# A decoder mixer kernel: the first merge gate computed as two sets of seven block products, with sums of weight blocks made by accumulating transfers

## Chip, cores and metric

The kernel runs on one core of a Trainium2 chip. Its time is the device time of one execution in microseconds (us), and lower is better. Three runs of the kernel before gave a median of 1141.31 us (1141.27 to 1141.62).

## The reference, cut to what matters

One decoder layer on 256 tokens of width 2048. The normed input is projected by `w_in`; the columns give a gated linear attention (q, k, v, gate), a differential attention (q, k, v, gate) and two merge gates `m_a` and `m_b`. Everything is float32.

```python
h = rmsnorm(x, pre_norm_g[l])
proj = h @ w_in[l]
(a_q, a_k, a_v, a_g, a_lr, b_q, b_k, b_v, b_g, m_a, m_b) = jnp.split(proj, offsets, axis=-1)
...                                     # o_a, o_b: the two mixers' gated outputs, 256 x 2048 each
y_a = o_a @ w_branch_a[l]
y_b = o_b @ w_branch_b[l]
merged = jax.nn.sigmoid(m_a) * y_a + jax.nn.sigmoid(m_b) * y_b
out = merged @ w_out[l]
x = x + rmsnorm(out, post_norm_g[l])
```

The change concerns `m_a = h @ W` with W of 2048 x 2048, four column groups of 512 named m00 to m03.

## The kernel before

All weights are read once from DRAM, in one flat array `w` laid out in the order of use (`chunk_plan`). A load brings 1 MB (128 partitions x 2048 numbers) into one of three `raw` buffers, issued on SP's queue. Each half of it (1024 numbers a partition) is a *unit*: ScalarE rounds it to fp32r (`hi`, L162), VectorE subtracts to get the rest (`lo`, L163), both into rings of three buffers. TensorE then computes three products for each block of 128 rows: x_hi·w_hi, x_lo·w_hi and x_hi·w_lo. x is split once into the `xs` tiles and stays.

`take` hands TensorE the next unit and keeps the splits and their loads up to AHEAD = 4 units in front. `token_major` (L304) computes a group of 512 columns for all 256 tokens: x blocks are the stationary operand, the weights stream by 512 columns, 8 steps of 12 matmuls into two PSUM banks (one for each 128 tokens). Work of other kinds (the two attentions, transposes) is written as generators in `tasks`; `pump` puts a piece of them between steps. A scheduler at build time then fixes each engine's order. Instructions of one engine run in that order, and so do SP's transfers: a transfer that waits for a buffer holds all behind it.

The order of the stages is: values v, keys and queries of the linear attention, its gate `ag`, the heads of the differential attention 0 and 1 (`diff_heads`), then for each g the gate m0g and the branch product y0g, heads 2 and 3, the gate groups m10 to m13, y10 to y13 (which read the attention outputs `obh` and `obl`, the hi and lo parts), then o0 to o3. Before, m0 and y0 make `part` (L771). After y1g VectorE forms (1 + tanh)·y_b + part in the gate's tile (L800, L801), and `turn` (L784) transposes it (L791) for the output product. Long-lived tiles come from one pool `big` of 4 KB slots that are reused in turn. GpSimd computes the attention's small rsqrt (`de`, L248) and a few memsets (L607).

Of the kernel before, what the change touches and what calls it, by code (L numbers as in the profile page):

```python
# [6 lines left out]
F32 = mybir.dt.float32  # L7
# [23 lines left out]
def chunk_plan():  # L31

    plan = []
    at = 0
    for g, n in enumerate(VG):
        if g == 0:
            plan.append(("v0", "two", "w_in", [(6144, RANK), (2048, 2 * n - RANK)]))
            at = 2 * n - RANK
        elif g > 1:
            plan.append((f"v{g}", "tok", "w_in", [(2048 + at, n)]))  # L40
            at += n
    for hf in range(2):
        for name, base in (("k", 1024), ("q", 0)):
            for c in range(4):
                plan.append((f"{name}{hf}{c}", "chan", "w_in", [(base + 512 * hf + P * c, P)]))
    for g in range(4):
        plan.append((f"ag{g}", "tok", "w_in", [(4096 + 512 * g, 512)]))
    o = 6144 + RANK

    def heads(g):  # L50
        plan.append((f"dv{g}", "tok", "w_in", [(o + 4096 + 512 * g, 512)]))
        plan.append((f"bg{g}", "tok", "w_in", [(o + 6144 + 512 * g, 512)]))
        for pair in range(2):
            for n, name in enumerate(("dq", "dk")):
                for c in (2 * pair, 2 * pair + 1):
                    plan.append((f"{name}{g}{c}", "chan", "w_in", [(o + 2048 * n + 512 * g + P * c, P)]))

    def gate(br, g):
        plan.append((f"m{br}{g}", "tok", "w_in", [(o + 8192 + 2048 * br + 512 * g, 512)]))

    def branch(br, g):
        plan.append((f"y{br}{g}", "tok", ("w_branch_a", "w_branch_b")[br], [(512 * g, 512)]))

    heads(0)
    heads(1)
    for g in range(4):
        gate(0, g)
# [7 lines left out]
    for g in range(4):  # L75
        plan.append((f"o{g}", "tok", "w_out", [(512 * g, 512)]))
    return plan


@with_exitstack  # L80
def hybrid_kernel(ctx: ExitStack, tc, xt, xn, preg, postg, w, w2, gkb, glag, lamv, diffg, ident_d, causal_d, lmask_d, out):
# [22 lines left out]

    def ps(tag):
        count[0] += 1
        return psum.tile([P, 512], F32, tag=tag, name=f"{tag}_{count[0]}")

    def f32(ap):
        return ap.bitcast(F32)  # L110


    plan = chunk_plan()
    halves = []
    off = 0
    for key, kind, _, cols in plan:
        n = sum(c for _, c in cols)
        size = ROWS[kind] * n
        for _ in range(KT // ROWS[kind]):
            halves += [(key, off, size, 0), (key, off, size, 1)]  # L120
            off += size * P
    ready = {}
    emitted = [0]
    raws = {}

    def emit_half():
        j = emitted[0]
        emitted[0] += 1
        key, at, size, h = halves[j]
        if h == 0:  # L130
            raws[at] = wpool.tile([P, 2048], F32, tag="raw", name=f"raw_{at}")
        raw = raws[at]
        src = w[at : at + P * size].rearrange("(p n) -> p n", p=P)
        n = size // 2
        early = key == "v0"
        if h == 0:
            if j == 0:
                load_x(0, 1)
            cuts = (0, n, size) if j == 0 else (0, size)
            for a, b in zip(cuts, cuts[1:]):  # L140
                i = sp.dma_start(raw[:, a:b], src[:, a:b])
# [11 lines left out]
        if key == "o3" and j + 1 < len(halves):  # L153
            hi_t, lo_t = u([P, 1024], "keep", F32R), u([P, 1024], "keep", F32R)
        else:
            hi_t = wpool.tile([P, 1024], F32R, tag="hi", name=f"hi_{j}")
            lo_t = wpool.tile([P, 1024], F32R, tag="lo", name=f"lo_{j}")
        fine = 2 if j == 0 else 1
        for i in range(fine):
            a, b = n * i // fine, n * (i + 1) // fine  # L160
            r = raw[:, n * h + a : n * h + b]
            act.activation(hi_t[:, a:b], r, AF.Copy)  # L162
            dve.tensor_tensor(out=lo_t[:, a:b], in0=r, in1=f32(hi_t[:, a:b]), op=ALU.subtract)  # L163
        ready[j] = (key, hi_t, lo_t)
# [3 lines left out]
    def take(key):  # L168
        j = used[0]
        used[0] += 1  # L170
        while emitted[0] < min(j + 1 + AHEAD, len(halves)):
# [130 lines left out]
        return i.ins  # L302

    def token_major(key, n, ops, step=1, groups=1):  # L304
        banks = [[ps(tag), ps(tag)] for tag in ("mm", "bg")[:groups]]
        spots = [(g, b) for g in range(groups) for b in range(2)]
        rows = 2 // groups
        for q in range(KT // rows):
            hi, lo = take(key)
            for w, parts in ((hi, (0, 1)), (lo, (0,))):  # L310
                for j in range(rows):
                    kt = rows * q + j
                    a = ops(kt)
                    for g, b in spots:
                        c = n * (groups * j + g)
                        for part in parts:
                            first, last = kt == 0 and w is hi and part == 0, kt == KT - 1 and w is lo
                            i = pe.matmul(banks[g][b][:, :n], a[part][:, P * b : P * b + P], w[:, c : c + n], start=first, stop=last)  # L318
            latest[0] = i.ins
            if groups == 1 and q % 2:  # L320
                pump(step)
            if groups == 2 and q == KT - 4:
                with tc.issue_after(latest[0]):
                    norm()
            if groups == 2 and q > 10:
                pump()
        return banks if groups == 2 else banks[0]

    def channel_major(key):
# [265 lines left out]


    obh, obl = [], []

    def diff_split(g, pair, tq, tk, q2, kh, kl):
        for m in range(2):  # L600
# [74 lines left out]
    def diff_attention():  # L675
# [3 lines left out]
        while n < 16 or last or pair:  # L679
# [24 lines left out]
                act.activation(new["wt"], new["bank"][:, :384], AF.Copy)  # L704
            if pair:
                split_out(bank, hi, lo, diffg_s)
                pair = None
            if last:
                if last["h"] % 2 == 0:
# [5 lines left out]
            if n == 16:  # L715
                yield

    def diff_heads(g):
# [8 lines left out]
        obh.append(u([P, 4, S], "obh", F32R))  # L727
        obl.append(u([P, 4, S], "obl", F32R))
        for pair in range(2):
            ts = []  # L730
            for name in ("dq", "dk"):
                t = t2([P, 2, S], name)
# [18 lines left out]
    def b_ops(kt):  # L751
        return obh[kt // 4][:, kt % 4, :], obl[kt // 4][:, kt % 4, :]

    def merge_gate(br, g, dst):
        banks = token_major(f"m{br}{g}", 512, x_ops, 1 + br)
        for b in range(2):
            act.activation(dst[:, b, :], banks[b], AF.Tanh, scale=half_rstd[:, b : b + 1])

    tasks.append(diff_attention())
    diff_heads(0)  # L760
# [1 line left out]

    while not {"out0", "out1"} <= done:
        pump()
    part = [u([P, 2, 512], "part") for _ in range(4)]
    for g in range(4):
        t = u([P, 2, 512], "mgate")
        merge_gate(0, g, t)
        banks = token_major(f"y0{g}", 512, a_ops)
        for b in range(2):  # L770
            dve.scalar_tensor_tensor(out=part[g][:, b, :], in0=t[:, b, :], scalar=1.0, in1=banks[b], op0=ALU.add, op1=ALU.mult)  # L771

    diff_heads(2)
    diff_heads(3)

    gb = [u([P, 2, 512], "gateb") for _ in range(4)]
    for g in range(4):
        merge_gate(1, g, gb[g])
    while tasks:
        pump()  # L780
    mh = [u([P, 4, S], "mh", F32R) for _ in range(4)]
    ml = [u([P, 4, S], "ml", F32R) for _ in range(4)]

    def turn(g):  # L784
        yield
        for i in range(2):
            bank = ps("bg")
            for j in range(2):
                for b in range(2):
                    c = P * (2 * i + j)  # L790
                    pe.transpose(bank[:, P * (2 * j + b) : P * (2 * j + b) + P], gb[g][:, b, c : c + P], ident)  # L791
            hi = mh[g][:, 2 * i : 2 * i + 2, :].rearrange("p a t -> p (a t)")
            lo = ml[g][:, 2 * i : 2 * i + 2, :].rearrange("p a t -> p (a t)")
            split_out(bank, hi, lo, 0.5)

    for g in range(4):
        banks = token_major(f"y1{g}", 512, b_ops)
        for b in range(2):
            t = gb[g][:, b, :]
            dve.scalar_tensor_tensor(out=t, in0=t, scalar=1.0, in1=banks[b], op0=ALU.add, op1=ALU.mult)  # L800
            dve.tensor_tensor(out=t, in0=t, in1=part[g][:, b, :], op=ALU.add)  # L801
        tasks.append(turn(g))
# [135 lines left out]
```

## Time and profile before

| what | value |
|---|---|
| median of three runs | 1141.31 us |
| profiled execution, span | 1139.5 us; its time outside the span is not recorded |
| TensorE, matmul / weight load | busy 1127.4 / 971.0 us, 5698 each |
| VectorE / ScalarE / GpSimd | busy 700.7 / 602.5 / 49.1 us |
| DMA | 211.60 MB, 53.2% of the 16 engines' span on SP's queue |

A matmul's busy time overlaps with that of its neighbours, so the time of one is read from the length of a long piece of the chain divided by its count. In the page's groups a row gives line, engine, operation, out<-in, count, busy us, mean ns of one, and then the idle time ahead of it with the engine it waited for.

### The profile page before, as it was taken

What the parts mean: (1) busy time and instruction counts of PE and PEld (TensorE: products, weight loads), DVE (VectorE), ACT (ScalarE), POOL (GpSimd) and SP (SyncE); (2) the same over time, 40 slices, a digit from 0 to 9 for tenths busy, and PEclk for the clock granted to TensorE, in tenths of its full rate; (3) what the DMA queues carried; (4) which work ended last, traced back from release to release, by engine and by line L of the source; (5) the groups of instructions that cost most, each with busy time, mean ns of one, the idle gap of its engine ahead of it and who ended that gap; (6) DMA issues with size and microseconds to landing.
All of it is one profiled execution on the core that took longest, in us unless ns stands there. A gap on an engine that the chain in (4) does not pass through costs nothing.

```text
span 1139.5 us, 14734 instructions
## 1 busy us (share of the span) xinstructions
PE 1127.4 (99%) x5698; PEld 971.0 (85%) x5698; DVE 700.7 (61%) x1025; ACT 602.5 (53%) x902; POOL 49.1 (4%) x61
## 2 busy tenths in 40 slices
PE   9999999999999999999999999999999999999997
PEld 8999888888888888888888888888888888888886
DVE  7765588657857766766444454676577544566454
ACT  7675454545646665665444434576466544444451
POOL 0100031001100000000000000000000000000000
PEclk9999999999999999999999999999999999999999
DMA  8756555545455445545555555554554555556762
GB/s 320 228 187 222 185 173 174 197 164 192 141 181 183 147 154 181 185 148 185 185 189 201 200 185 188 187 180 148 185 185 148 174 196 185 185 188 207 275 217 74
DMA packets 32742, 211.60 MB, mean 186 GB/s; under 512 B 4192, under 2 KB 4832, under 8 KB 10144
## 3 DMA queue, kind: packets, MB, share of 16 engines
q1 hardware_dynamic: 31952, 209.61, 53.2%
q10 hardware_dynamic: 720, 1.06, 0.3%
q8 instruction: 44, 0.72, 0.3%
q14 instruction: 26, 0.21, 0.1%
HBM read 208.55 MB, written 2.10 MB: 185 GB/s over the span
## 4 chain that ended last, share of the span: by engine, by line
PE 97%; issue 1%; ACT 1%; DMA 0%; DVE 0%; SPq 0%; DVEq 0%; POOLq 0%; POOL 0%; ACTq 0%
PE mm L318 65%; PE mm L339 15%; PE mm L341 8%; PE bg L318 1%; PE mm L301 1%; PE bg L508 1%; PE bg L301 1%; PE bg L624 1%; PE bg L625 1%; DMA raw<-in_w_dram 0%; PE bg L650 0%; ACT kh L605 0%; PE bg L791 0%; PE bg L577 0%; ACT kh L604 0%
## 5 line engine op out<-in xcount | busy, mean ns | idle before, releaser
L163 DVE TENSOR_TENSOR lo<-raw,hi 128x1024 fp32r<-128x1024 f32 (+3 forms) x386 | 467.7, 1214 | 347.3 <-ACT hi L162 344.4
L162 ACT ACTIVATE hi<-raw 128x1024 fp32r<-128x1024 f32 (+3 forms) x386 | 401.5, 1042 | 459.3 <-PE mm L318 338.3
L318 PE MATMUL mm<-hi,xs 128*128 128x512 f32 (+2 forms) x1536 | 373.0, 384 | 1.4 <-ACT hi L162 1.4
L318 PEld LDWEIGHTS mm<-hi,xs 128*128 128x128 f32 x1536 | 285.6, 188 | 50.6 <-ACT hi L162 2.0
L318 PE MATMUL mm<-lo,xs 128*128 128x512 f32 (+2 forms) x768 | 201.5, 382 | 0.0
L339 PE MATMUL mm<-xs,hi 128*128 128x512 f32 x768 | 195.6, 393 | 0.0
L318 PEld LDWEIGHTS mm<-lo,xs 128*128 128x128 f32 x768 | 143.8, 188 | 25.6 <-DVE lo L163 0.3
L339 PEld LDWEIGHTS mm<-xs,hi 128*128 128x128 f32 x768 | 138.4, 189 | 24.2
L341 PEld LDWEIGHTS mm<-xs,lo 128*128 128x128 f32 x768 | 104.8, 190 | 7.5
L341 PE MATMUL mm<-xs,lo 128*128 128x256 f32 x768 | 107.1, 282 | 0.0
L318 PE MATMUL mm<-hi,obh 128*128 128x512 f32 x128 | 50.1, 391 | 0.0
L318 PE MATMUL mm<-hi,oah 128*128 128x512 f32 x128 | 49.9, 390 | 0.0
L318 PE MATMUL mm<-hi,obl 128*128 128x512 f32 x128 | 49.8, 389 | 0.0
L318 PE MATMUL mm<-hi,oal 128*128 128x512 f32 x128 | 49.8, 389 | 0.0
L635 ACT ACTIVATE prob<-prob,mx,score_scale 128x128 f32<-128x128 f32 x64 | 34.3, 537 | 7.8 <-DVE mx L630 7.2
L318 PE MATMUL mm<-hi,mh 128*128 128x512 f32 x96 | 37.5, 390 | 0.0
L318 PE MATMUL mm<-hi,ml 128*128 128x512 f32 x96 | 37.4, 389 | 0.0
L318 PE MATMUL mm<-lo,oah 128*128 128x512 f32 x128 | 34.2, 389 | 0.0
L318 PE MATMUL mm<-lo,obh 128*128 128x512 f32 x128 | 34.2, 389 | 0.0
L248 POOL TENSOR_TENSOR de<-de,neg_half 128x2 f32<-128x2 f32 x16 | 11.8, 738 | 395.8 <-DVE de L669 395.8
L318 PEld LDWEIGHTS mm<-lo,oah 128*128 128x128 f32 x128 | 24.0, 188 | 5.0
L318 PEld LDWEIGHTS mm<-lo,obh 128*128 128x128 f32 x128 | 24.0, 188 | 5.0
(194 smaller groups left out, 984.9 us busy)
## 6 DMA issues: line engine op xcount, KB each, us to landing
raw<-in_w_dram SPq DMA_DIRECT2D x176, 1024.0 KB, 4.9
raw<-in_w_dram SPq DMA_DIRECT2D x15, 832.0 KB, 6.4
raw<-in_w_dram SPq DMA_DIRECT2D x4, 800.0 KB, 4.5
xres<-in_xn_dram SPq DMA_DIRECT2D x4, 512.0 KB, 10.2
xraw<-in_xt_dram SPq DMA_DIRECT2D x3, 512.0 KB, 8.0
lmask<-in_lmask_dram SPq DMA_DIRECT2D x2, 512.0 KB, 7.6
pg<-in_postg_dram SPq DMA_DIRECT2D x2, 512.0 KB, 6.7
out_dram<-yg SPq DMA_DIRECT2D x4, 256.0 KB, 2.7
```

The lines of the kernel that those rows point to most:

```text
L162: act.activation(hi_t[:, a:b], r, AF.Copy)
L163: dve.tensor_tensor(out=lo_t[:, a:b], in0=r, in1=f32(hi_t[:, a:b]), op=ALU.subtract)
L248: pool.tensor_tensor(out=dst, in0=src, in1=neg_half[:, : src.free_size()], op=ALU.pow)
L301: i = pe.matmul(out, lhs, rhs, start=first and n == 0, stop=last and n == len(pairs) - 1)
L318: i = pe.matmul(banks[g][b][:, :n], a[part][:, P * b : P * b + P], w[:, c : c + n], start=first, stop=last)
L339: i = pe.matmul(o, hi[:, c], x_pair(kt), start=kt == 0, stop=kt == KT - 1)
L341: i = pe.matmul(o[:, :S], lo[:, c], x_ops(kt)[0], start=False, stop=False)
L508: pe.matmul(o, xk[:, P * c : P * c + P], xq.rearrange("p (b c t) -> p b c t", b=2, c=4)[:, :, c, :], start=i == 0, stop=i == 1)
L624: pe.matmul(banks[m][:, lo:up], q2[:, m, i2, t], kh[:, m, i2, :n], start=True, stop=False)
L625: pe.matmul(banks[m][:, lo:up], q2[:, m, i2, t], kl[:, m, i2, :n], start=False, stop=True)
L635: act.activation(prob[m][:, lo:up], prob[m][:, lo:up], AF.Exp, scale=score_scale[:, b : b + 1], bias=mx[:, i : i + 1], accum_out=z[:, i : ...
```

## The change

The gate m0 is no longer computed group by group. Two column groups form a *set* of 1024 columns. The weights of a set are cut into 2 x 2 blocks of 1024 rows x 512 columns, x into 2 x 2 blocks of 128 tokens x 1024 channels, and the 2 x 2 block product is formed by seven block products in place of eight (`PRODUCTS`). Each product is four units of 1024 numbers with 6 matmuls a unit, all into one bank.

The seven need sums of x blocks and of weight blocks. The x sums are made once on VectorE and split (`block_operands`, a task during the last heads). The weight sums are made in memory: two *chains* of four tiles. A chain tile is loaded from DRAM by SP; after its unit was split, a transfer issued by GpSimd adds the next weight block onto it (`accum_op=ALU.add`). Chain 0 serves products 1, 3, 5 and 7, chain 1 products 2 and 6, and in the second set the two swap. Product 4 uses a plain block, loaded as two raw tiles. A transfer is issued eight units ahead (`load_block(i + 8)`). Results of the products are combined on VectorE and ScalarE (`block_set`), and the two sets' 56 steps are interleaved with the 32 steps of m10 to m13 (`schedule`, `mixed`).

With the gate moved behind the heads, y0g is computed by itself and copied to `part` by ScalarE; the tiles `part`, `obh` and `obl` are written to DRAM by GpSimd's queue and read back by SP before y1. `part` is multiplied by the gate just after y1's products. All PSUM tiles now share one ring of eight banks, `big` has 34 slots, and the memory that GpSimd's transfers use for their descriptors is set to 4096 bytes.

```diff
-    big = ctx.enter_context(tc.tile_pool(name="big", bufs=32))
+    big = ctx.enter_context(tc.tile_pool(name="big", bufs=34))
...
-    psum = ctx.enter_context(tc.tile_pool(name="psum", bufs=4, space=bass.MemoryType.PSUM))
+    psum = ctx.enter_context(tc.tile_pool(name="psum", bufs=8, space=bass.MemoryType.PSUM))
+    dram = ctx.enter_context(tc.tile_pool(name="dram", bufs=1, space=bass.MemoryType.DRAM))
...
+    first = order.index("m10")
+    regular(*order[:first])
+    mixed((0, 1), *(f"m1{g}" for g in range(4)))
+    regular(*(f"y1{g}" for g in range(4)), *(f"o{g}" for g in range(4)))
...
+PRODUCTS = (
+    ("a11", 0, (0, 0), False),
+    ("s4", 1, (1, 1), False),
+    ("s1", 0, (0, 1), True),
+    ("a12", None, (1, 0), False),
+    ("n2", 0, (1, 1), True),
+    ("n7", 1, (0, 1), True),
+    ("a22", 0, (1, 0), True),
+)
...
+    def load_block(i):
+        if i < len(set_steps):
+            chain, src, adds = block_unit(i)
+            if adds:
+                pool.dma_start(chain, src, accum_op=ALU.add)
+            elif chain is not None:
+                sp.dma_start(chain, src)
...
+            act.activation(hi_t, raw, AF.Copy)
+            dve.tensor_tensor(out=lo_t, in0=raw, in1=f32(hi_t), op=ALU.subtract)
+            load_block(i + 8)
...
+                    for t, far in ((obh[g], obh_far[g]), (obl[g], obl_far[g])):
+                        pool.dma_start(far, f32(t))
...
+        def product_of(slot, bank, first):
+            operand = squares[PRODUCTS[slot][0]]
+            for unit in range(4):
+                hi, lo = take((n, 4 * slot + unit))
+                for wt, parts in ((hi, (0, 1)), (lo, (0,))):
+                    for j in range(2):
+                        kt = 2 * unit + j
+                        a = operand(kt)
+                        for part in parts:
...
+                            i = pe.matmul(bank, a[part], wt[:, 512 * j : 512 * j + 512], start=go, stop=end, skip_group_check=not first)
...
+        banks = token_major(f"y0{g}", 512, a_ops, 2)
+        t = u([P, 2, 512], "part")
+        for b in range(2):
+            act.activation(t[:, b, :], banks[b], AF.Copy)
+        pool.dma_start(part_far[g], t)
...
+    lanes = {True: set_gates(), False: group_gates()}
+    at = used[0]
+    for key, _ in steps[at : at + 56 + 32]:
+        next(lanes[isinstance(key, int)])
...
+        sp.dma_start(f32(obh[g]), obh_far[g])
+        sp.dma_start(f32(obl[g]), obl_far[g])
...
+        sp.dma_start(part[g], part_far[g])
...
+        dve.scalar_tensor_tensor(out=part[g], in0=gates[0][g], scalar=1.0, in1=part[g], op0=ALU.add, op1=ALU.mult)
```

What the scheduler makes of it shows at three places. First TensorE's order at the end of y13, before (mm_8483 is y13's bank, mm_8669 and mm_8670 o0's, gateb_7290 the tile of gate 3; repeated rows are left out):

```order
L318 MATMUL mm_8483<-lo_8537,obh_6822 128x512
L318 MATMUL mm_8669<-hi_8568,mh_8020 128x512
L318 MATMUL mm_8669<-hi_8568,ml_8024 128x512
L318 MATMUL mm_8670<-hi_8568,mh_8020 128x512
L318 MATMUL mm_8670<-hi_8568,ml_8024 128x512
L318 MATMUL mm_8669<-lo_8569,mh_8020 128x512
L318 MATMUL mm_8670<-lo_8569,mh_8020 128x512
L791 MATMUL bg_8638<-ident,gateb_7290 128x128
L791 MATMUL bg_8645<-ident,gateb_7290 128x128
```

Eleven matmuls of o0 stand between y13's last and the first transposes. Now (mm_8679 and mm_8680 are y13's banks, mm_8867 and mm_8868 o0's, mgate_8175 the tile of gate 3):

```order
L426 MATMUL mm_8679<-lo_8734,obh_8193 128x512
L426 MATMUL mm_8680<-lo_8734,obh_8193 128x512
L1036 MATMUL bg_8836<-ident,mgate_8175 128x128
L1036 MATMUL bg_8843<-ident,mgate_8175 128x128
L426 MATMUL mm_8867<-hi_8765,mh_8214 128x512
L426 MATMUL mm_8867<-hi_8765,ml_8218 128x512
L426 MATMUL mm_8868<-hi_8765,mh_8214 128x512
L426 MATMUL mm_8868<-hi_8765,ml_8218 128x512
```

The first two transposes have moved ahead of all of o0. Second, SP's order; before, this queue holds the raw tiles alone here (these are the last of m13 and the first of y10):

```order
L141 DMA raw_42500096_8030<-in_w_dram 128x2048
L141 DMA raw_42762240_8064<-in_w_dram 128x2048
L141 DMA raw_43024384_8098<-in_w_dram 128x2048
L141 DMA raw_43286528_8132<-in_w_dram 128x2048
L141 DMA raw_43548672_8172<-in_w_dram 128x2048
```

Now, first around product 4 of set 0 (raw_s0 are its two tiles, raw_m1 those of the other gate), and then from m13's last tile on:

```order
L241 DMA raw_m10_4_6975<-in_w_dram 128x2048
L241 DMA raw_m10_6_7050<-in_w_dram 128x2048
L219 DMA raw_s0_12_7123<-in_w_dram 128x2048
L219 DMA raw_s0_14_7163<-in_w_dram 128x2048
L241 DMA raw_m11_0_7178<-in_w_dram 128x2048
```

```order
L241 DMA raw_m13_6_8066<-in_w_dram 128x2048
L241 DMA raw_y10_0_8135<-in_w_dram 128x2048
L241 DMA raw_y10_2_8157<-in_w_dram 128x2048
L241 DMA raw_y10_4_8224<-in_w_dram 128x2048
L1022 DMA obh_606_8190<-obh_far_151_2512 128x1024
L1023 DMA obl_610_8194<-obl_far_155_2516 128x1024
L1022 DMA obh_607_8191<-obh_far_152_2513 128x1024
L1023 DMA obl_611_8195<-obl_far_156_2517 128x1024
```

Raw tiles take the three buffers in this order, so raw_m11_0 gets the buffer of raw_m10_6 and raw_y10_4 that of raw_m13_6, and the attention outputs come back behind raw_y10_4. Third, GpSimd's order during the heads' end, before:

```order
L248 TENSOR_TENSOR de_526_7361<-de_526_7361,neg_half_114 128x2
L248 TENSOR_TENSOR de_539_7478<-de_539_7478,neg_half_114 128x2
L248 TENSOR_TENSOR de_556_7607<-de_556_7607,neg_half_114 128x2
L248 TENSOR_TENSOR de_560_7656<-de_560_7656,neg_half_114 128x2
L248 TENSOR_TENSOR or_628_9170<-or_628_9170,neg_half_114 128x1
```

Now, in the first half of the mixed stage (L202 are the adds onto the chain tiles):

```order
L202 DMA chain0_490_6493<-in_w_dram 128x1024
L348 TENSOR_TENSOR de_560_7093<-de_560_7093,neg_half_116 128x2
L202 DMA chain0_491_6494<-in_w_dram 128x1024
L202 DMA chain0_488_6491<-in_w_dram 128x1024
L202 DMA chain0_489_6492<-in_w_dram 128x1024
L348 TENSOR_TENSOR de_580_7308<-de_580_7308,neg_half_116 128x2
L202 DMA chain0_490_6493<-in_w_dram 128x1024
L202 DMA chain0_491_6494<-in_w_dram 128x1024
```

The attention's rsqrt stands between and behind adds that each wait for a split.

More of the change, by code (lines that the diff above doesn't have):

```diff
@@ L75, in chunk_plan, with units, schedule, regular @@
     for g in range(4):
+        gate(0, g)
+    for g in range(4):
         plan.append((f"o{g}", "tok", "w_out", [(512 * g, 512)]))
     return plan
+def units(kind):
+    return 2 * KT // ROWS[kind]
+def schedule():
+    kinds = {key: kind for key, kind, _, _ in chunk_plan()}
+    steps = []
+    def regular(*keys):
+        steps.extend((key, n) for key in keys for n in range(units(kinds[key])))
+    def mixed(sets, *keys):
+        s = [(i, n) for i in sets for n in range(SLOTS * 4)]
+        at = len(steps)
+        regular(*keys)
+        r = steps[at:]
+        del steps[at:]
+        i = j = 0
+        while i < len(s) or j < len(r):
+            if j == len(r) or (i < len(s) and i * len(r) <= j * len(s)):
+                steps.append(s[i])
+                i += 1
+            else:
+                steps.append(r[j])
+                j += 1
+    order = [key for key, _, _, _ in chunk_plan()]
+    first = order.index("m10")
+    regular(*order[:first])
+    mixed((0, 1), *(f"m1{g}" for g in range(4)))
+    regular(*(f"y1{g}" for g in range(4)), *(f"o{g}" for g in range(4)))
+    return steps
+SLOTS = 7
+SETS = (("m00", "m01"), ("m02", "m03"))
+PRODUCTS = (
[7 more added lines that the diff above has]
+)
 @with_exitstack
@@ L106, in ps, with away @@
         count[0] += 1
-        return psum.tile([P, 512], F32, tag=tag, name=f"{tag}_{count[0]}")
+        return psum.tile([P, 512], F32, tag="bank", name=f"{tag}_{count[0]}")
+    def away(shape, name, dtype=F32):
+        count[0] += 1
+        return dram.tile(shape, dtype, tag=f"{name}_{count[0]}", name=f"{name}_{count[0]}", bufs=1)
     def f32(ap):
         return ap.bitcast(F32)
-    plan = chunk_plan()
-    halves = []
+    steps = schedule()
+    kinds, sizes, begins = {}, {}, {}
     off = 0
[L116 to L121, printed above, removed]
+    for key, kind, _, cols in chunk_plan():
+        kinds[key] = kind
+        sizes[key] = ROWS[kind] * sum(c for _, c in cols)
+        begins[key] = off
+        off += KT // ROWS[kind] * sizes[key] * P
     ready = {}
@@ L124, in hybrid_kernel, with piece, block_unit @@
     raws = {}
+    chains = [[], []]
+    set_steps = [step for step in steps if not isinstance(step[0], str)]
+    def piece(key, q):
+        size = sizes[key]
+        at = begins[key] + q * size * P
+        return w[at : at + P * size].rearrange("(p n) -> p n", p=P)
+    def block_unit(i):
+        n, step = set_steps[i]
+        slot, unit = divmod(step, 4)
+        _, chain, (kh, g), adds = PRODUCTS[slot]
+        if chain is not None:
+            chain = chains[(chain + n) % 2][unit]
+        src = piece(SETS[n][g], 2 * kh + unit // 2)[:, 1024 * (unit % 2) : 1024 * (unit % 2) + 1024]
+        return chain, src, adds
+    def load_block(i):
[5 more added lines that the diff above has]
+                sp.dma_start(chain, src)
     def emit_half():
@@ L304, in token_major, with token_steps @@
     def token_major(key, n, ops, step=1, groups=1):
+        run = token_steps(key, n, ops, step, groups)
+        while True:
+            try:
+                next(run)
+            except StopIteration as e:
+                return e.value
+    def token_steps(key, n, ops, step=1, groups=1):
         banks = [[ps(tag), ps(tag)] for tag in ("mm", "bg")[:groups]]
@@ L729, in diff_heads @@
         for pair in range(2):
+            before_pair(pair)
             ts = []
@@ L752, in b_ops, with x_square, ops @@
         return obh[kt // 4][:, kt % 4, :], obl[kt // 4][:, kt % 4, :]
[L754 to L757, printed above, removed]
+    squares = {}
+    def x_square(half, kh):
+        def ops(kt):
+            hi, lo = x_ops(8 * kh + kt)
+            c = slice(P * half, P * half + P)
+            return hi[:, c], lo[:, c]
+        return ops
```

155 lines of the change are left out of this document (133 added, 22 removed).

## The prediction

> **What bounds the kernel now.** I read the page first: the busy shares, the slices and the chain of waits.
>
> ```profile
> span 1139.5 us, 14734 instructions
> PE 1127.4 (99%) x5698; PEld 971.0 (85%) x5698; DVE 700.7 (61%) x1025; ACT 602.5 (53%) x902; POOL 49.1 (4%) x61
> ...
> PEclk9999999999999999999999999999999999999999
> ...
> PE 97%; issue 1%; ACT 1%; DMA 0%; DVE 0%; SPq 0%; DVEq 0%; POOLq 0%; POOL 0%; ACTq 0%
> ```
>
> TensorE carries 97% of the chain at the full granted clock. A matmul removed is time gained only if nothing else comes to stand in its place, so the question is what a matmul costs, and how near the other resources are in the stages that the change rebuilds. The chain in order of time gives the first:
>
> ```profile
> 532.59 179.57 PE mm L318 x792
> ...
> 904.10 81.66 PE mm L318 x360
> ...
> 1109.15 10.89 PE mm L301 x48
> ```
>
> The first piece is the m0 and y0 stage: 179.57 / 792 = 0.2267 us for one matmul of 512 columns. The second is in the m1 stage, 0.2268. The third (o3) adds 48 matmuls in a row into one bank, as the new products will, at 0.2269. I use 0.2268. The groups and the waits say who feeds TensorE:
>
> ```profile
> L163 DVE TENSOR_TENSOR lo<-raw,hi 128x1024 fp32r<-128x1024 f32 (+3 forms) x386 | 467.7, 1214 | 347.3 <-ACT hi L162 344.4
> L162 ACT ACTIVATE hi<-raw 128x1024 fp32r<-128x1024 f32 (+3 forms) x386 | 401.5, 1042 | 459.3 <-PE mm L318 338.3
> ```
> ```profile
> PE mm L318 <- ACT hi L162: 1.4, 2, 0.9
> ```
>
> Each unit of weights is split by ScalarE (1.04 us) and VectorE (1.21 us). They wait 338 and 344 us for TensorE or for each other, and TensorE waits 1.4 us for them: there is room. Windows of the two stages that matter (columns: length, then PE, PEld, DVE, ACT, POOL busy with counts, clock, DMA share, GB/s), then a window of the loading at the start, where one queue fills all 16 engines, and two rows of DMA issues:
>
> ```profile
> 765.00:905.00 140.00, 138.46 (x736) 118.69 (x736) 91.04 (x189) 86.56 (x165) 7.85 (x12) 1.00 0.50 169
> 904.00:986.00 82.00, 82.00 (x365) 67.87 (x365) 39.73 (x36) 36.00 (x37) 0.00 (x0) 1.00 0.55 192
> ```
> ```profile
> DMA packets 830, 4.25 MB, mean 425 GB/s; under 512 B 88, under 2 KB 88, under 8 KB 830
> ...
> q1 hardware_dynamic: 830, 4.25, 102.0%
> ```
> ```profile
> raw<-in_w_dram SPq DMA_DIRECT2D x176, 1024.0 KB, 4.9
> ...
> pg<-in_postg_dram SPq DMA_DIRECT2D x2, 512.0 KB, 6.7
> ```
>
> The m1 stage leaves 45% of the DMA engines idle. Saturated they move 425 GB/s, so 1 MB (1.049 million bytes) holds them 2.47 us and half of it 1.23 us. A raw load lands 4.9 us after its issue, 2.4 us more than its bytes take.
>
> **The change, part by part.** *Matmuls.* A gate group is 8 steps of 12 matmuls, four groups 384. A set is 7 products x 4 units x 6 = 168, two sets 336. 48 go: 48 x 0.2268 = **-10.9 us**, all on the chain. I expect no slower pace, by the o3 row.
>
> *Splits.* The gate's 32 splits become 56: +24 x 1.04 = 25.0 us of ScalarE, +24 x 1.21 = 29.1 us of VectorE. What hides them is the mixed stage: 336 + 384 = 720 matmuls, 163.3 us. In it VectorE has 88 x 1.214 + 12 sums of 0.69 = 115 us and ScalarE 88 x 1.042 + 16 tanh and 4 copies of about 0.68 = 105 us, plus the end of the attention. Step by step it is tighter: a set step lasts 6 x 0.2268 = 1.36 us against VectorE's 1.21, an m1 step 2.72. At 56 to 32 the mean is 1.86. Cost 0, with little slack wherever attention puts its own work between.
>
> *Operand blocks.* 16 adds (under 0.69 each, below), 4 differences and 4 splits at 1.21: at most 20.7 us of VectorE and 4.2 of ScalarE, in the stage 765 to 905, where VectorE is busy 91 of 140. Cost 0; without that cover it would be the 20 us.
>
> *Transfers of the mixed stage.* Plain: 16 raw tiles of m1, 4 of the fourth products, about 2 of y10 ahead, less some 2 loaded before the stage: 20 x 2.47 = 49.4 us of the engines; 8 chain loads of set 1, 9.9 us; 4 attention stores, 4.9 us. Together 64 us. Accumulating: 32 of 512 KB, 39.5 us if they cost what a copy costs. No row shows one. Call the ratio to a copy r. The lower bound is r = 1. An add onto what is there reads the target besides the source and writes it once, so r = 2 is the nearest reading: 79 us, and 143 of 163 us in all. If the two reads and the write of a row run one after the other, where a copy's read and write overlap, it is r = 3, my upper bound: 118 us, and 182 of 163. The stage becomes DMA-bound at (163.3 - 64) / 39.5 = **r = 2.5**. I take r = 2 and cost 0, because an add's two reads are the only bytes more than in the rows above; both ends stay in the range. [...]
>
> *Time for an add to land.* A chain tile is refilled when its unit is split and is needed eight set steps later: 8 x 163.3 / 56 = 23 us. Three products in a row (third, fifth, sixth) trigger adds: 12 adds in 12 set steps of 2.92 us with their share of m1, 35 us; with r = 2 that is 30 us of engines beside 13 us of plain loads (3.4 tiles of m1, two of the fourth product): late by 8, inside the 23.
>
> *GpSimd's queue.* It issues the 32 adds, each waiting for a split of VectorE, with the attention's rsqrt between and behind them.
>
> ```profile
> L248 POOL TENSOR_TENSOR de<-de,neg_half 128x2 f32<-128x2 f32 x16 | 11.8, 738 | 395.8 <-DVE de L669 395.8
> ...
> L607 POOL MEMSET kl<- 64x512 f32 x16 | 8.3, 521 | 94.4 <-DVE part L771 93.6
> ```
> ```profile
> 1029.84 0.33 SPq L141 DMA_DIRECT2D raw<-in_w_dram  x1
> ```
>
> How long GpSimd takes to issue a transfer no row shows: 0.33 us as on SP, to some 1 us (twice a memset). 12 in 35 us could cost 2.9 each before the queue is late. A late rsqrt delays the attention's last outputs, which are wanted only by y1. Cost 0.
>
> *Raw tiles.* Three raw buffers serve m1 and the fourth product, which takes two of them in each set. The m1 load queued behind these (raw_m11_0 in set 0, raw_m13_0 in set 1) reuses the buffer of the m1 tile just split, so it can start only after that split. The next m1 split is due one m1 step and 1.75 set steps later, 2.72 + 1.75 x 1.36 = 5.1 us; the load lands in 4.9 alone, so the lower bound is 0. If adds share the engines evenly its bytes take twice as long: 4.9 + 2.47 = 7.4, late by 2.3, twice, 4.6 in all. I take 1 us each: **+2.0**.
>
> *Attention outputs and parts.* 12 stores and 12 loads of 512 KB. The stores lie in stages at half DMA share, cost 0. The loads stand on SP behind raw_y10_4, which waits for the buffer of m13's last tile. When that is split, TensorE has the steps left that the three hi buffers allow: about 5.0 us (a set step of 1.36, an m13 step of 2.72, part of the set steps before). The first output pair lands after 2.47 + 1.23 + 2.4 = 6.1 and 2.47 + 2 x 1.23 + 2.4 = 7.3 us. TensorE has two matmuls (0.45) between the two: 7.3 - 5.0 - 0.45 = **+1.8**. Bounds: 0, if SP gets past its wait 2 us earlier, and 4, if the half-megabyte loads land like pg's (6.7 where its own bytes take 1.23). The other ten come while TensorE works, 2.5 us a pair, and a pair serves 24 matmuls or 5.4 us.
>
> *The last turn.* Before, TensorE goes from y13 into eleven matmuls of o0, and only then to the transposes of gate 3:
>
> ```profile
> L801 DVE TENSOR_TENSOR gateb<-gateb,part 128x512 f32<-128x512 f32 x8 | 5.5, 686 | 0.0
> ...
> L800 DVE SCALAR_TENSOR_TENSOR gateb<-gateb,mm 128x512 f32<-128x512 f32 x8 | 5.5, 683 | 4.3 <-PE mm L318 4.3
> ```
> ```profile
> 1043.27 1.22 DVE L163 TENSOR_TENSOR lo<-raw,hi 128x1024 fp32r<-128x1024 f32 x1
> ...
> 1044.41 0.68 DVE L801 TENSOR_TENSOR gateb<-gateb,part 128x512 f32<-128x512 f32 x1
> ...
> 1045.24 0.41 PE L791 MATMUL bg<-ident,gateb 128*128 128x128 f32 x2
> ```
>
> The split and the add before the first transposes ran behind those matmuls. Now the transposes stand right behind y13's last matmul, and wait for 683 + 1214 + 686 ns = 2.58 of VectorE, less some overlap: **+2.5**. The lower bound is 0 only if VectorE takes the sum before the split, which its order does not say.
>
> **Sum:** -10.9 + 2.0 + 1.8 + 2.5 = -4.6 us against the profiled span of 1139.5, so 1134.9. The span is 1.8 below the runs' median of 1141.3, which I keep: **1136.7**. The terms' ends: -10.9 + 0 + 0 + 2.5 = -8.4 (1132.9) below; above, with the raw term at its end, -10.9 + 4.6 + 1.8 + 2.5 = -2.0 (1139.3), and with the reload's too 1141.5. Its own range is 1133 to 1139.
>
> **Rivals.** *Slower: the adds bound the mixed stage.* At r = 3 the engines need 182 us in a stage of 163: 19 us more in place of a gain, 1141.3 - 4.6 + 19 = 1156. At r = 4 it is 222 us: 1195. It decides at r = 2.5; there the result is 1137 to 1141, and each 0.1 of r above costs 4 us. For it: no row shows an add, the slack at r = 2 is 12%, and lateness of a chain tile stops TensorE directly. Against: 45% idle engines, and 23 us of lead.
>
> *No change: GpSimd issues too slowly.* If an issue takes 1 us and waits out two VectorE splits of 1.21 besides, 3.4 us, the run of 12 needs 41 of 35 us and ends 6 us late. The chain tiles don't notice, with 23 us of lead, but the rsqrt does, and attention matmuls stand in TensorE's order between the products. If a third of it reaches TensorE in each set, that is 4 us: 1140.7. It decides from 35 / 12 = 2.9 us an issue. The memset row speaks against it: GpSimd writes 64x512 in 521 ns on the mean, beside a VectorE that is 61% busy. [...]
>
> *The full gain.* If the raw, reload and turn terms are all hidden: 1130.4. The turn row makes that unlikely.
>
> **Chances.** The forecast with its ends (to 1139) 0.50; nearer the full gain, below 1133, 0.08; no change (r near 2.5, or GpSimd) 0.15; slower 0.27. A measurement of this kernel can tell 0.2% or 2.3 us, so faster is 0.58, within 0.15, slower 0.27. The range reaches from the low end, 1133, to r = 3 with a little, 1157; beyond it lie 0.05 below and about 0.13 above.
>
> **What would show it.** 5650 matmuls; the mixed stage 163 us long with TensorE at 98% or more; waits of TensorE for hi (L262, after raw_m11_0 and raw_m13_0) of about 1 us each, for obh at y10 of 1.8, for VectorE at the last transposes of 2.5. An add of 512 KB should land in under 8 us and GpSimd's queue share be near twice a copy's. I am wrong if TensorE waits in the set products (L930) for the split of a chain tile that waits for a GpSimd transfer, again and again: then r is above 2.5 and the time above 1141.

## The result and the profile after

The changed kernel takes **1150.09 us** (median of five runs, 1146.37 to 1151.84) against 1141.27 for the kernel before (1141.05 to 1141.62): ratio 1.0068, 95% interval [1.0049, 1.0086]. By that ratio it is 0.7% slower (the medians alone give 1.0077), where 0.4% faster was forecast. The time lies inside the wide range that was stated (1133 to 1157), but far above the ends of the forecast's own sum (1133 to 1139). The profiled execution is the one of 1150.09, and its span is 8.8 us above that of before. First the page of the changed kernel: busy time, two rows of the slices, and the shares of the chain.

```profile
span 1148.3 us, 14907 instructions
PE 1125.1 (98%) x5650; PEld 966.7 (84%) x5650; DVE 748.3 (65%) x1081; ACT 635.6 (55%) x942; POOL 84.1 (7%) x105
...
PEclk9999999999999999999999999999999899999999
DMA  8756555545454454456665555858899969657552
...
PE 89%; DMA 3%; ACT 2%; DVE 2%; issue 2%; POOL 0%; SPq 0%; DVEq 0%; POOLq 0%; ACTq 0%
```

The 48 matmuls are gone, but TensorE has 89% of the chain where it had 97%. Two signs tell where to look: transfers have 3% of the chain, where they had none, and the granted clock has an 8 in its 32nd slice. The chain in order of time (start, length, piece) names the places:

```profile
815.37 7.19 DMA raw_m<-in_w_dram
823.75 3.06 PE mm L426 x12
...
901.71 9.09 DMA raw_m<-in_w_dram
911.99 5.49 PE mm L426 x12
...
950.08 6.54 DMA obl<-obl_far
956.66 1.68 PE mm L426 x6
960.43 12.10 DMA raw_y<-in_w_dram
```

Four transfers now stand in the chain: the first tiles of m11 and m13, the lo part of the first attention output, and a tile of y1 queued behind the reloads. The piece at 911.99 is odd in another way: 12 matmuls take 5.49 us, where 12 x 0.2268 = 2.72 are due. Then the waits of TensorE (total us, times, longest) and the DMA issues (median from issue to landing):

```profile
PE mm L426 <- ACT hi L262: 9.4, 5, 3.6
PE bg L1036 <- DVE mgate L1047: 2.4, 1, 2.4
PE bg L736 <- ACT kh L717: 1.6, 4, 0.7
...
PE mm L426 <- DMA obl<-obl_far: 0.5, 1, 0.5
```
```profile
raw_m<-in_w_dram SPq DMA_DIRECT2D x16, 1024.0 KB, 7.4
chain<-in_w_dram POOLq DMA_DIRECT2D x32, 512.0 KB, 10.9
```

The wait for hi was 1.4 us before and is 9.4; a raw tile of m1 lands after 7.4 us, not 4.9. One of the five waits for hi, 1.04 us ahead of y10, is put down to the wrong cause: it ends at 955.49 us, right after obh landed (issued at 949.56, landed at 955.35), while the split of that unit was done at 951.0. No row says that a set product (L930) waits. What ScalarE did at the two raw tiles (in brackets its idle time and what ended it):

```profile
822.64 1.06 ACT L262 ACTIVATE hi<-raw_m 128x1024 fp32r<-128x1024 f32 x1 [3.78 <-DMA raw_m<-in_w_dram]
```
```profile
910.88 1.06 ACT L262 ACTIVATE hi<-raw_m 128x1024 fp32r<-128x1024 f32 x1 [4.07 <-DMA raw_m<-in_w_dram]
```

And the clock: windows of 3.41 us (length, PE busy, PEld, DVE, ACT, POOL with counts, granted clock, DMA share, GB/s), set on the moments at which the trace shows the clock change:

```profile
818.81:822.22 3.41, 1.64 (x8) 1.02 (x6) 0.00 (x0) 0.05 (x1) 0.00 (x0) 1.00 1.01 424
...
907.56:910.97 3.41, 0.83 (x4) 0.37 (x2) 0.00 (x0) 0.09 (x1) 0.00 (x0) 1.00 1.03 362
910.97:914.39 3.42, 2.40 (x6) 1.92 (x7) 2.42 (x3) 2.86 (x3) 0.00 (x0) 0.50 0.40 164
914.39:917.80 3.41, 3.41 (x10) 2.64 (x9) 1.30 (x2) 1.06 (x1) 0.00 (x0) 0.50 0.71 233
917.80:921.21 3.41, 3.41 (x17) 2.79 (x16) 2.22 (x2) 1.91 (x3) 0.87 (x1) 1.00 0.96 372
1047.51:1050.92 3.41, 1.07 (x6) 0.96 (x7) 3.38 (x5) 0.14 (x1) 0.00 (x0) 1.00 0.85 335
1050.92:1054.33 3.41, 3.41 (x13) 2.81 (x12) 1.38 (x3) 1.19 (x2) 0.00 (x0) 0.50 1.01 352
```

After the pause at 908 and the one at the last turn, TensorE ran at half its clock for 6.83 and 3.41 us: the window from 914.39 us counts 10 matmuls, the next one, at full clock, 17. After the pause at 820 it did not. The matmuls' starts in the two traces, stage by stage, give the whole difference:

| where | us |
|---|---|
| 48 matmuls less | -10.9 |
| pauses at m11 and m13 (3.47 and 3.76) | +7.2 |
| half clock after m13's pause | +2.8 |
| pauses at y10 and behind the reloads (1.20, 0.64, 1.08, smaller ones) | +3.1 |
| pause at the last turn | +2.5 |
| half clock behind it | +1.6 |
| attention's own small pauses (460 to 815 us) | +1.0 |
| start: full clock from 9.85 us, before from 5.28 | +1.0 |
| the rest | +0.4 |
| sum, and the difference of the spans | +8.7, +8.8 |

The row of the start is put down to chance: in kernels below, whose programs begin alike, the full clock is recorded from 4.9 us (all three edits) and from 9.60 us (the reloads moved).

### The profile page after: what moved, and what is told of

The parts are those of the page before. It is cut to its first block, busy times and chain, and to the rows that moved or that the text cites. A ratio compares the mean times of both kernels' runs of the same rounds, so it can differ in the third digit from the quotient of the medians.

```text
span 1148.3 us, 14907 instructions
## 1 busy us (share of the span) xinstructions
PE 1125.1 (98%) x5650; PEld 966.7 (84%) x5650; DVE 748.3 (65%) x1081; ACT 635.6 (55%) x942; POOL 84.1 (7%) x105
## 3 DMA queue, kind: packets, MB, share of 16 engines
q10 hardware_dynamic: 720, 1.06, 0.3%
## 4 chain that ended last, share of the span: by engine, by line
PE 89%; DMA 3%; ACT 2%; DVE 2%; issue 2%; POOL 0%; SPq 0%; DVEq 0%; POOLq 0%; ACTq 0%
PE mm L426 55%; PE mm L449 15%; PE mm L451 7%; PE set L930 5%; PE bg L426 2%; DMA raw_m<-in_w_dram 1%; DMA raw_y<-in_w_dram 1%; PE mm L401 1%; PE bg L618 1%; ACT hi L262 1%; DVE lo L263 1%; PE bg L401 1%; PE bg L736 1%; DMA obl<-obl_far 1%; PE bg L737 1%
## 5 line engine op out<-in xcount | busy, mean ns | idle before, releaser
L426 PE MATMUL mm<-hi,xs 128*128 128x512 f32 (+2 forms) x1280 | 312.0, 385 | 7.5 <-ACT hi L262 7.5
L426 PEld LDWEIGHTS mm<-hi,xs 128*128 128x128 f32 x1280 | 239.7, 189 | 48.0 <-ACT hi L262 8.6
L263 DVE TENSOR_TENSOR lo<-raw_y,hi 128x1024 fp32r<-128x1024 f32 x64 | 78.1, 1225 | 63.2 <-ACT hi L262 62.6
L262 ACT ACTIVATE hi<-raw_y 128x1024 fp32r<-128x1024 f32 x64 | 67.6, 1060 | 88.8 <-PE mm L426 77.3
L224 DVE TENSOR_TENSOR lo<-chain,hi 128x1024 fp32r<-128x1024 f32 x48 | 58.6, 1223 | 17.8 <-ACT hi L223 17.1
L223 ACT ACTIVATE hi<-chain 128x1024 fp32r<-128x1024 f32 x48 | 50.8, 1061 | 27.9 <-PE set L930 19.4
L263 DVE TENSOR_TENSOR lo<-raw_bg,hi 128x1024 fp32r<-128x1024 f32 x32 | 39.2, 1224 | 30.8 <-ACT hi L262 30.8
L263 DVE TENSOR_TENSOR lo<-raw_ag,hi 128x1024 fp32r<-128x1024 f32 x32 | 41.2, 1289 | 27.2 <-ACT hi L262 27.2
L263 DVE TENSOR_TENSOR lo<-raw_v,hi 128x832 fp32r<-128x832 f32 (+2 forms) x41 | 41.0, 1015 | 20.5 <-ACT hi L262 20.2
L263 DVE TENSOR_TENSOR lo<-raw_dk,hi 128x1024 fp32r<-128x1024 f32 x32 | 39.2, 1224 | 22.3 <-ACT hi L262 22.0
## 6 DMA issues: line engine op xcount, KB each, us to landing
chain<-in_w_dram POOLq DMA_DIRECT2D x32, 512.0 KB, 10.9
```

The source lines that it names most:

```text
L223: act.activation(hi_t, raw, AF.Copy)
L224: dve.tensor_tensor(out=lo_t, in0=raw, in1=f32(hi_t), op=ALU.subtract)
```

## The experiments

Theory A: each pause has a cause of its own (the three raw buffers under the adds' load; the order on SP's queue; the order at the last turn), and a pause that leaves TensorE idle for most of a 3.41 us window halves its clock for the next one or two (above, two after a window with 0.83 us busy, one after 1.07). Gains below are differences of the ratios to the kernel before (the changed kernel's is 1.0068), times 1141; by the two intervals each is good to some 2 us.

**Tiles of its own for the fourth product.**

```diff
-  raws[key] = wpool.tile([P, 2048], F32, tag="raw", ...)
-  sp.dma_start(raws[key], piece(...))
+  for m in range(2):
+      raws[key, m] = u([P, 1024], "raw_s")
+      sp.dma_start(raws[key, m], src[:, 1024 * m : 1024 * m + 1024])
```

> The fourth product's weights get four tiles of their own in the big pool instead of two of the three raw buffers; nothing else is changed. Theory A (the ring of three raw buffers makes m11's and m13's first loads start late, and the second of the two pauses drops the clock): the pauses of 3.47 and 3.76 us at these two steps fall to under 0.5 each, the half clock at 911 to 918 us goes with them, in all 7 + 3 = 10 us: about 1140. Rival B (the adds' traffic makes every load late, wherever it is put): the first loads of m11 and m13 still land late, the pauses stay at 2 us or more each, and the time stays above 1145.

1139.86 us, ratio 0.998 [0.9971, 0.9988]: 10 us gained. A window of the mixed stage in the changed kernel, the same one here, and the wait for hi here:

```profile
790.00:940.00 150.00, 143.09 (x636) 117.67 (x635) 100.66 (x116) 93.65 (x120) 26.94 (x32) 0.98 0.95 263
```
```profile
790.00:940.00 150.00, 149.99 (x681) 124.36 (x681) 109.18 (x123) 100.65 (x127) 26.94 (x32) 1.00 0.94 265
```
```profile
PE mm L428 <- ACT hi L264: 2.4, 3, 1.0
```

45 more matmuls pass in the same 150 us, though the DMA engines are as full (0.94) and a raw tile lands even later (9.1 us in this window, 8.0 in the changed kernel). So it was not the load as such but the lack of a buffer in which to start early. SP's rows for the four tiles of m11, in the changed kernel and here, show the start:

```profile
815.37 12.21 SPq L241 DMA_DIRECT2D raw_m<-in_w_dram  x4
```
```profile
797.02 24.95 SPq L243 DMA_DIRECT2D raw_m<-in_w_dram  x4
```

m11's first tile takes 14.2 us to land here, twice as long as the 7.19 of the changed kernel, but it is issued 18 us earlier. m13's is issued 25 us earlier (876.88 against 901.71) and takes 13.6.

**Plain copies for the adds.**

```diff
-  pool.dma_start(chain, src, accum_op=ALU.add)
+  pool.dma_start(chain, src)
```

> The 32 accumulating transfers are plain copies of the same blocks to the same tiles on the same queue, so that the products multiply single blocks and not sums. Theory A (the ring of buffers lets the raw load of m11 and m13 start late, and the adds, at 328 ns a row of 4 KB against 159, stretch its landing from 4.9 to 7 and 9 us): with copies it lands in 5 to 6 us, the pauses fall to 1 to 1.5 us each, the clock stays full: 1150.1 - 4.5 - 3 = about 1142.5. Rival B (VectorE's and ScalarE's splits are late there because of the attention, and the adds hardly matter): the pauses stay at 3 us or more each and the time within 2 us of 1150.

1140.35 us, ratio 0.9987 [0.9978, 0.9996]: 9.2 us gained. The same window, and GpSimd's queue in it (packets, MB, share of 16 engines) in the changed kernel and here:

```profile
790.00:940.00 150.00, 149.00 (x675) 123.21 (x675) 107.68 (x122) 99.56 (x126) 17.79 (x32) 1.00 0.74 258
```
```profile
q0 software_dynamic: 4645, 16.87, 55.2%
```
```profile
q0 software_dynamic: 4256, 15.48, 29.0%
```

With copies the first tiles of m11 and m13 are issued about as late as in the changed kernel (814.57 and 898.60 us), but they land after 4.88 and 4.92 us, not 7.19 and 9.09. The pauses are 1.15 us at m11 and none at m13; the DMA share falls from 0.95 to 0.74. Either remedy alone does away with the 7.2 us (all of it, or 6.0) and with the half clock behind: both causes are needed, the late start and the slow landing.

**The last turn among the first matmuls of o0.**

```diff
         tasks.append(turn(g))
-    while tasks:
-        pump()
```

> The last turn is left in the list of tasks, so that its transposes are issued behind the first matmuls of o0 and not right behind y13; nothing else is changed. Theory A (a pause of 2.55 us there, and the half clock for 3.41 us behind it that costs some 1.2 us): 1150.1 - 3.7 = about 1146.4, the pause under 0.5 and the clock full from there to the end. Rival B (the pause only moves: the first products of o0 that need this turn wait for it): a new pause of 1 us or more in o0 and no gain over 1 us.

1145.12 us, ratio 1.0032 [1.0021, 1.0043]: 4.1 us gained. The row of waits for mgate is gone, no pause stands in o0, and the trace shows full clock from 917.7 us to TensorE's last matmul.

**Reloads on GpSimd's queue.**

```diff
-        sp.dma_start(f32(obh[g]), obh_far[g])
-        sp.dma_start(f32(obl[g]), obl_far[g])
+        pool.dma_start(f32(obh[g]), obh_far[g])
+        pool.dma_start(f32(obl[g]), obl_far[g])
```

(and `part` likewise.)

> The twelve loads of the attention outputs and parts are issued on GpSimd's queue instead of SP's, where they stood behind a weight load that waits for its buffer and ahead of y10's and y11's; nothing else is changed. Theory A (the order on SP's queue is the cause): the pauses of 1.20, 0.64 and 1.08 us at y10 go, 2.9 in all: about 1147.2. Rival B (the loads wait for their target's tiles or for GpSimd's other work, or GpSimd's transfers land later than SP's): the first pause stays at 1 us or grows, and the time is 1149 or more.

1146.58 us, ratio 1.0046 [1.0032, 1.006]: 2.5 us gained. That alone is not clear of the noise, since the interval overlaps with the changed kernel's [1.0049, 1.0086]; the trace shows what happened. In the changed kernel SP issued the first reload at 949.56 us; here GpSimd does:

```profile
925.23 0.84 POOL L1022 DMA_DIRECT2D obh<-obh_far  x1
```

24 us earlier and behind no weight load; all three pauses at y10 and y11 are gone.

**Work added where TensorE pauses.**

```diff
+    def warm(n):
+        bank = ps("warm")
+        with tc.issue_after(latest[0]):
+            for _ in range(n):
+                latest[0] = pe.matmul(bank, x_ops(0)[0][:, :P], x_pair(0), start=True, stop=True).ins
...
         for g in range(4):
+            if g % 2:
+                warm(12)
...
+    warm(9)
     while tasks:
```

> Work is added and nothing taken away: 12 matmuls of 512 columns (2.7 us), whose result nobody reads, stand on TensorE right before m11 and before m13, and 9 (2.0 us) before the last turn, where it waits anyway. Theory A (a window of 3.41 us in which TensorE is busy for less than some third halves the clock for the next window or two): no half clock from 10 us to the end in any run, the time falls to 1145 to 1146.5 and the runs lie closer together. Rival B (the half clock has another cause, power or the DMA load): it stays at 911 us and the time is 1150 or more; if the pauses were not real idle time, 33 x 0.227 = 7.5 us more, 1157.

1145.27 us, ratio 1.0031 [1.0021, 1.0041]: 33 matmuls more, and 4.2 us *less*; this interval and the changed kernel's lie apart. Neither of the two half-clock stretches is there. The window ahead of m13 has the DMA engines as full as in the changed kernel (1.02, there 1.03), but TensorE busy for 3.41 us, not 0.83, and the next window keeps the full clock, so a full DMA load alone is not the cause:

```profile
907.00:910.41 3.41, 3.41 (x16) 2.52 (x14) 0.00 (x0) 0.30 (x1) 0.00 (x0) 1.00 1.02 369
```

The runs did not draw together, though (1143.06 to 1147.87), and the profiled one has a new stretch: the pause at y10, which was left in, grew to 2.08 and 0.59 us, and the clock fell behind it. The two windows there, three of the kernel with the reloads moved, and one of the kernel with the turn moved:

```profile
951.37:954.78 3.41, 1.47 (x5) 0.97 (x6) 1.56 (x2) 1.14 (x2) 0.00 (x0) 1.00 1.02 416
954.78:958.20 3.42, 3.42 (x9) 2.65 (x8) 0.09 (x1) 1.06 (x1) 0.00 (x0) 0.50 1.02 419
```
```profile
910.72:914.13 3.41, 2.87 (x7) 2.30 (x8) 2.89 (x3) 2.38 (x3) 0.00 (x0) 0.50 0.23 94
914.13:917.55 3.42, 3.42 (x17) 2.78 (x16) 1.83 (x2) 2.03 (x2) 0.21 (x1) 1.00 0.83 297
1040.43:1043.84 3.41, 1.68 (x8) 1.06 (x6) 2.33 (x4) 1.06 (x1) 0.00 (x0) 1.00 0.57 171
```
```profile
910.89:914.31 3.42, 2.71 (x6) 2.16 (x7) 2.73 (x3) 2.56 (x3) 0.00 (x0) 0.50 0.24 98
```

In these rows and the changed kernel's, every window at full clock with TensorE busy for 1.47 us or less is followed by half the clock, none with 1.64 or more; windows laid in the same way through the whole traces of the changed kernel and the one before give no exception, nor do those read in others (0.37 us with the reloads moved, 0.22 with the storage alone and 1.03 with tiles for the fourth product, each followed by half the clock; 1.74 with plain copies, not). The way back is less sharp: a window at half clock with 2.87 busy ended it, those with 2.40 and 2.71 did not. But at the start of the kernel with the reloads moved, a window with 2.91 busy (2.78 to 6.19 us) did not bring the full clock either, which is recorded from 9.60 us on; in the changed kernel one with 2.82 (3.03 to 6.44 us) did not, and in the one before one with 2.98 (1.87 to 5.28 us) did. So TensorE's busy time by the profile does not settle where that border lies. In the kernel with the reloads moved, the same 2.5 us pause at the last turn fell across two windows (1.68 busy in the first) and cost no clock.

**Storage in DRAM alone.** The first gate in its regular groups, no sets, no adds; everything else as changed. Then the same with the turn and the reloads mended:

```diff
-    mixed((0, 1), *(f"m1{g}" for g in range(4)))
+    regular(*(f"m0{g}" for g in range(4)), *(f"m1{g}" for g in range(4)))
```

> The attention outputs and parts go through DRAM and the first gate comes behind the attention, as in the changed kernel, but it is computed in the regular four groups: no sets of block products, no adds. Theory A (the price of the storage is on SP's queue at y10, some 3 us, and that of the last turn 2.5 us with some 1 us of clock): 1141.3 + 6.5 = about 1148. Rival B (these pauses come from the traffic of the adds just ahead of them): within 2 us of 1141.3, or the turn alone, 1144.

> The kernel of e7_far with the two edits of e2_turn and e3_reload. Theory A: its two pauses go and it takes what the kernel before takes, 1141 to 1142; e5_all is 48 x 0.2268 = 10.9 us below it, the worth of the block products by themselves. Rival B (the order of the stages or the stores cost time of their own): 1144 or more. If the block products are worth less than their matmuls, e5_all is less than 9 us below it.

The first takes 1151.95 us, ratio 1.009 [1.0075, 1.0106], dearer than the 1148 expected. Its largest wait:

```profile
PE mm L426 <- DMA obh<-obh_far: 5.1, 1, 5.1
```

Without set steps behind m13's last tile, TensorE comes to y10 sooner after SP gets past its wait, 0.6 us behind the issue of the first reload (952.38 us) where it was 4.7 in the changed kernel: a pause of 5.24 us, and half the clock for 6.83 behind it. So this storage costs more where no sets stand. Mended it takes 1140.71, ratio 0.9992 [0.9983, 1.0001]: the order of the stages and the stores cost nothing that can be measured.

**All three edits.**

> The three edits of e1_raw, e2_turn and e3_reload together. Theory A (three pauses, each with its own cause, and the half clock that follows two of them): the gains add up, 1150.1 - 10.2 - 5.0 - 3.5 = about 1131.5, 10 below the kernel before, which is what the 48 matmuls are worth; the clock stays full, TensorE's waits behind the set products are under 0.5 us each. Rival B (a pause taken away shows the next one behind it, on the queues that are now busier at the same time): 1135 or more, with new waits of over 1 us at y10 or y11.

1131.98 us (1131.79 to 1132.41), ratio 0.9915 [0.9901, 0.9928]. All that TensorE waits for in this kernel:

```profile
PE bg L738 <- ACT kh L719: 1.6, 4, 0.7
PE mm L428 <- ACT hi L264: 1.3, 2, 0.8
PE bg L338 <- DVE ones L335: 1.0, 1, 1.0
```

The clock is full from 4.9 to 1124.5 us. This version beats both kernels: 9.7 us below the one before. Against the mended storage alone it is 8.7 us lower, not 10.9, and less than the 9 us set as the mark: the block products are worth less than their matmuls. In the traces 1.5 of the missing 2.2 are attention pauses between 460 and 790 us, mainly 0.92 and 0.32 at 781, where TensorE waits for ScalarE's `kh`. ScalarE had itself sat idle for VectorE's `dk`, which stands behind the split of a set unit (L226):

```profile
777.22 1.22 DVE L226 TENSOR_TENSOR lo<-chain,hi 128x1024 fp32r<-128x1024 f32 x1
778.35 0.42 DVE L857 TENSOR_TENSOR dk<-dk,rstd_bc 128x256 f32<-128x256 f32 x1
```
```profile
778.80 0.63 ACT L718 ACTIVATE kh<-dk 64x512 fp32r<-64x512 f32 x1 [1.28 <-DVE dk L857]
```

That is a reading of the two traces; no run took it away.

**Copies for the adds, with buffers enough.** The adds of the last kernel as plain copies, and that kernel once more beside it.

> The kernel of e5_all with the 32 accumulating transfers as plain copies, so that the products multiply single blocks and not sums. Theory A (the adds' traffic does harm only through the ring of three raw buffers, and costs nothing once the fourth product has tiles of its own): within 1 us of e5_all, 1131 to 1133. Rival B (the traffic costs time of its own, by late chain tiles or a slower SBUF): 3 us or more below it, under 1129.

> The kernel of e5_all once more, on the same chip as e9_all_plain, so that the two can be set side by side: 1131 to 1133 by both theories.

1131.55 us, ratio 0.9912 [0.9898, 0.9925], and 1132.3, ratio 0.9915 [0.9901, 0.9929]: no difference that the intervals can tell. The adds' traffic, which costs 9 us with three raw buffers, costs nothing measurable once the fourth product has tiles of its own.

## Why the prediction was wrong, step by step

The span is 13.4 us above the forecast one (1148.3 against 1134.9). Of this, 5.2 us are the raw tiles, 4.4 the clock and 1.3 the reloads; the start, the attention's pauses and the rest make 2.4. Two steps failed: the raw term was too small, and the clock had no term.

- *Matmuls, -10.9.* Right as a count; set products run at the pace taken (12 in 2.72 us). Cleared of the three pauses the change is worth 8.7 us against the mended storage.
- *Raw tiles, +2.0.* This step failed: 7.2. The mechanism and both places were right. At m11 the load was issued 4.9 us before TensorE was ready (5.1 predicted) and landed in 7.19 (7.4 at the upper end); but the working ended with the landing, and ScalarE's split of 1.06 us comes after it: 7.19 + 1.06 - 4.9 = 3.4. At m13 it was issued 6.5 us ahead and took 9.09: "shared evenly" was no upper bound. And between the ends 1 was taken, although the prediction's own sum had the engines 143/163 = 88% full (0.95 measured between 790 and 940 us), where the raw tiles of m1 landed after 8.0 us in the median and not after 4.9.
- *The clock.* This step failed too: missing altogether, +4.4. The waits were priced at their length only. In the trace of the changed kernel the stretches of full and half clock between 9.85 and 1143.08 us are whole multiples of 3.413 us (264, 2, 39, 1 and 26 of them), and a window need not be empty to be followed by half the clock: 0.83, 1.07 and even 1.47 us of work in one did not save it. The same 2.5 us pause at the last turn cost 1.6 us more here (1.07 us busy in its window) and nothing with the reloads moved, where it fell across two windows (1.68 in the first). So a pause need not cost its second price in every run; that fits the 1146.4 to 1151.8 of the changed kernel, whose two shortest times have a mean granted clock of 0.996 and the others 0.991 to 0.993.
- *Reload, +1.8.* Right (1.20 + 0.64). Left out was what is queued behind: twelve reloads held SP, y1's tile landed after 12.10 us, and TensorE paused another 1.08.
- *Last turn, +2.5.* Right: 2.55. Its rows in the changed kernel are the ones forecast:

```profile
1047.28 0.69 DVE L1046 SCALAR_TENSOR_TENSOR mgate<-mgate,mm 128x512 f32<-128x512 f32 x1 [1.08 <-PE mm L426]
1047.88 1.22 DVE L263 TENSOR_TENSOR lo<-raw_o,hi 128x1024 fp32r<-128x1024 f32 x1
1049.02 0.69 DVE L1047 TENSOR_TENSOR mgate<-mgate,part 128x512 f32<-128x512 f32 x1
```

- *Adds, r = 2.* Right: the median packet of 4 KB takes 328 ns in an add and 159 in a copy, 2.06. By the queue rows above, 150 x 0.552 / 16.87 = 4.9 us a MB against 150 x 0.29 / 15.48 = 2.8, 1.75 with the stores that share the queue. "Lands in under 8 us" was wrong (10.9), but the lead covered it: from an add's issue to ScalarE's split of its tile the trace has 19.1 us at least (23 predicted), every add had landed 10.6 us or more before that split, and no set product waited.
- *GpSimd's queue.* Right: an add's issue took 0.87 us (0.86 to 0.94 for the 32), a lone plain transfer 0.54 (a store of `obl`, at 855.91 us), far from 2.9.
- *Splits and operand blocks, 0.* Nearly: some 1 us of attention pauses, at the places of which the prediction had said that there is little slack.
- *The rivals.* The slower case came in, but by another mechanism than the one named: the adds did not bound the mixed stage; they made two raw tiles late. A rival of that kind, pauses plus the clock, had not been given. The sign named for being wrong, TensorE waiting in the set products, did not show, and yet the time is above 1141. That it lies within 1133 to 1157 is luck: the upper end was set for r = 3, an assumption of the author that no run shows, and r came out near 2 (2.06).

## What to carry to other kernels

When a ring of buffers gets a second user, count from the moment a buffer comes free to the end of the step that follows the landing, with the landing time of the loaded stage; a burst deserves tiles of its own, and then the same traffic costs nothing measurable (10 us gained here). Put loads that only fetch stored results on a queue where they stand behind no wait for a buffer. Price a pause of TensorE twice: its length, and, where it can empty most of a 3.41 us window (1.47 us busy or less here), 1.6 to 2.8 us more of half clock; useless matmuls in the gap can even pay (33 of them, 4.2 us less).

## What the runs showed of the hardware

- Work put into a pause made a kernel faster: 33 matmuls more, 4.2 us less.
- Half the clock came after a 3.41 us window with TensorE busy for 1.47 us or less and after none with 1.64 or more. On the way back, windows with 2.40 and 2.71 us busy did not bring the full clock, one with 2.87 did, and one with 2.91 at a kernel's start did not.
- A 4 KB packet of an accumulating transfer took 328 ns of a DMA engine in the median, one of a copy 159 (changed kernel), and a 1 MB load beside a queue of such transfers landed after 9.1 us, not 4.9 (m13's first tile, 4.92 with copies and 9.09 with adds).
